# Two output blocks of the w_up product stay in PSUM for the convolution

## The chip, the cores and the metric

The kernel runs on one core of one Trainium2 chip. The time is device microseconds of one launch. TensorE (PE in the profile) multiplies into PSUM banks of 128 partitions by 512 words of fp32; VectorE (DVE), ScalarE (ACT) and GpSimd (POOL) do the rest of the arithmetic on SBUF and, the first two of them, on PSUM; SyncE (SP) issues DMAs.

## The reference

One layer of an encoder: two attentions, then a feed-forward part with a convolution over positions. Batch 1, 1024 positions, 1024 features, 2816 hidden features. The attentions are not touched by the change; the feed-forward part is:

```python
h2 = rmsnorm(x, g_ffn[i]) * (1 + scale2) + shift2
u = depthwise_conv_seq(h2 @ w_up[i], conv_w[i], conv_b[i])   # three taps over positions, 5632 channels
u_val, u_gate = jnp.split(u, 2, axis=-1)
x = x + gate2 * ((jax.nn.gelu(u_gate, approximate=True) * u_val) @ w_down[i])
return rmsnorm(x, g_final)
```

## The kernel before

Activations lie with features on partitions and positions along the free dimension. Every fp32 operand of the feed-forward part is held as two fp32r tiles, hi (rounded) and lo (the remainder), and a product is three matmuls: hi by hi, hi by lo, lo by hi.

`h2 @ w_up` is done in 22 tiles (`FF`, index t). A tile makes 128 value channels and the 128 gate channels that belong to them, at all 1024 positions: four blocks of 128 by 512, block (i, hf) with i = 0 for value, 1 for gate, and hf for the half of the positions. It is a 2 by 2 product in the Strassen-Winograd way: rows are value and gate, the inner index is cut in two halves of four k-tiles, columns are the position halves. So there are seven products instead of eight, in the order of `STEPS` (weights "11", S2, S1, S3, "12", S4, "22" by activations B11, T2, T1, T3, B21, B22, T4), each of 4 k-tiles by 3 matmuls, 84 matmuls a tile (L1204 to L1206 in `products`). "x" and "xb", "T2hi", "wsh", "whi" and the like in the trace are such operands; wsh and wsl are hi and lo of the summed weights S2, S1, S3.

The seven products go into four PSUM banks a, b, c, d (tag "pj", six in all, so the next tile starts in two others). What each step j does when its product is there:

- j = 0, bank a: copied to the SBUF temporary t (ScalarE, L1210); bank a goes on accumulating.
- j = 1, bank b: added to t (VectorE, L1212), which frees b.
- j = 2, bank c: c + t goes into the SBUF temporary v (L1214).
- j = 3, bank d: d + v is block (1, 1), gate, second half (L1217). It is written into v, in SBUF; d is then free.
- j = 4: bank a, with a second product added, is block (0, 0).
- j = 5: bank c with a second product, plus t, is block (0, 1), written in c (L1225).
- j = 6: bank d with a second product, plus t, is block (1, 0), gate, first half (L1229). It is written into t, in SBUF.

So the value row's two blocks are read by the convolution from PSUM, and the gate row's two from SBUF. The temporaries are of `wide()`, an SBUF pool of five tiles called "wc" in the trace.

Each block is handed to `done`. `conv_in` (ScalarE, L1420) starts a row's output y (a "big" tile) with the centre weight and the bias, 512 positions at a time; when both halves are there, `conv_taps` (VectorE, L1426) adds the two side weights in six multiply-adds: two of 512 elements, two of 256, two of 255. For a row whose halves are ph[0] and ph[1], three taps read each. With both rows done come the gelu (ScalarE, L1452), the product (VectorE, L1453) and the store to a DRAM scratch (L1454), from which w_down reads its operand later.

The weights of a tile are loaded two tiles ahead; `a_operands` forms their sums on GpSimd (L1154 to L1156) and one on VectorE (L1171), and splits them: hi on ScalarE (L57), lo on GpSimd (L61).

Two more PSUM banks, tags pcol and pbc, hold the column sums and the broadcast of the RMS norm before w_up (the broadcast, `bc`, is read last by `scale(6)`), and from the w_down stage on they are staging for its operands (`moved`, L1252, which cycles through the two by `stages`).

Tiles 0, 1 and 2 are special: the operand T2, T1, T3 and the others are still being made when they start, so their products run in the order 0, 4, 1, 2, 3, 5, 6 and are interleaved; the convolution of a row waits until both halves are there; tile 2 keeps t and block (0, 0) in two held SBUF tiles. In the last tile (t = 21) things differ too, and the change leaves it out.

The order of instructions on each engine, and which tile takes which buffer, is set when the program is built, by a planner that simulates the engines, except where the kernel is inside `manual_schedule`: there the code's own order holds (PE up to `late_mm.close()` after the first two advances of tiles 0 and 1; ScalarE, VectorE and GpSimd while the operands T2, T1, T3, B22, T4 are made). The taps and the additions of tiles 0 to 21 are outside of these, as is PE from `late_mm.close()` on.

Of the kernel before, what the change touches and what calls it, by code (L numbers as in the profile page):

```python
# [10 lines left out]
FT = mybir.dt.float32  # L11
# [9 lines left out]
FF = 22  # L21
# [8 lines left out]
def hybrid_encoder(tc, xT, c, w_ada, small, w_in, p1_bias, p23_bias, na_bias, ln2_mult, ident, w_br, w_out,  # L30
# [218 lines left out]
    def v_wide(*sts):  # L249
        ps = [ps_s.tile([128, 512], FT, name="pv", bufs=3) if len(sts) == 1 else ps_g.tile([128, 512], FT, name="pj")  # L250
              for _ in sts]
        for k in range(KT):
            whi, wlo = (t[:, :, k] for t in v_all)
            for st, p in zip(sts, ps):
                hhi, hlo = (t[:, st % 4 * 128:st % 4 * 128 + 128] for t in h[st // 4, k])
                pe.matmul(p, hhi, whi, start=k == 0, stop=False)
                pe.matmul(p, hhi, wlo, start=False, stop=False)
                pe.matmul(p, hlo, whi, start=False, stop=k == KT - 1)
        return ps
# [122 lines left out]
    with tc.manual_schedule(engines={e.engine for e in (sp, act, dve, pool, pe)}):  # L382
# [18 lines left out]
        stage = [None, first]  # L401
# [52 lines left out]
        stage = [ps_n.tile([128, 512], FT, name="pcol"), ps_s.tile([128, 512], FT, name="pv", bufs=3)]  # L454
# [45 lines left out]
        for n, step in enumerate(v_steps[:9]):  # L500
            if step is None:
# [3 lines left out]
                ps = [ps_g.tile([128, 512], FT, name="pj") for _ in range(2)]  # L505
# [9 lines left out]
            else:  # L515
                p = v_wide(*step[1:])
# [489 lines left out]
    with tc.manual_schedule(engines={e.engine for e in (pe, act, dve)}):  # L1006
        for s in range(101):
            n = 4 if s < 64 else 8 if s < 72 else 6 if s < 88 else 4
# [23 lines left out]
    ps = tc.alloc_tile_pool(name="ps", bufs=1, space=PSUM, reuse_waits="tile")  # L1032
# [29 lines left out]
    with tc.tile_pool(name="gate", bufs=1, reuse_waits="tile") as work:  # L1062
# [37 lines left out]
        for i in range(2 * KT):  # L1100
# [17 lines left out]
            p = []  # L1118
# [64 lines left out]
        pair(raw[0][:, 1:2], ("S4",), s4[:, 0:1], s4[:, 1:2])  # L1183
        yield

    def products(st, n, moving, done, seq=range(7), in_psum=False, hold=None):

        p, c = {}, {}

        def bank(x_):  # L1190
            p[x_] = ps.tile([128, 512], FT, name="pj", bufs=6)
            return p[x_]

        def tmp(x_):
            c[x_] = hold[0] if hold and x_ == "t" else wide()
            return c[x_]
        for j in seq:
            a, b = STEPS[j]
            x_ = "abcdacd"[j]
            psum = bank(x_) if j < 4 else p[x_]  # L1200
            whi, wlo = st[a]
            for k in range(n):
                bhi, blo = moving(b, k)
                pe.matmul(psum, whi[:, k], bhi, start=j < 4 and k == 0, stop=False, skip_group_check=True)  # L1204
                pe.matmul(psum, whi[:, k], blo, start=False, stop=False, skip_group_check=True)  # L1205
                pe.matmul(psum, wlo[:, k], bhi, start=False, stop=k == n - 1, skip_group_check=True)  # L1206
                if k < n - 1:
                    yield -1
            if j == 0:
                act.activation(tmp("t"), psum, AF.Copy)  # L1210
            elif j == 1:
                dve.tensor_tensor(c["t"], psum, c["t"], OP.add)  # L1212
            elif j == 2:
                dve.tensor_tensor(tmp("v"), psum, c["t"], OP.add)  # L1214
            elif j == 3:
                dst = p["b"] if in_psum else c["v"]
                dve.tensor_tensor(dst, psum, c["v"], OP.add)  # L1217
                done(1, 1, dst)
            elif j == 4 and hold:
                act.activation(hold[1], psum, AF.Copy)  # L1220
                done(0, 0, hold[1])
            elif j == 4:
                done(0, 0, psum)
            elif j == 5:
                dve.tensor_tensor(psum, psum, c["t"], OP.add)  # L1225
                done(0, 1, psum)
            else:
                dst = psum if in_psum else c["t"]
                dve.tensor_tensor(dst, psum, c["t"], OP.add)  # L1229
                done(1, 0, dst)  # L1230
            yield j
# [8 lines left out]
    def wide(dtype=FT):  # L1240
        return keep.tile([128, 512], dtype, name="wc", bufs=5)

    def big(shape, dtype=FT):
        return keep.tile(shape, dtype, name="big", bufs=9)
# [5 lines left out]
    stages = itertools.cycle(("pcol", "pbc"))  # L1250
# [136 lines left out]
    held = [up1.tile([128, 512], FT, name="held", bufs=2) for _ in range(2)]  # L1387
# [25 lines left out]
    with tc.tile_pool(name="up", bufs=2, reuse_waits="tile") as work:  # L1413
# [5 lines left out]
        def conv_in(y, t, hf, src):  # L1419
            act.activation(y[:, halves[hf]], src, AF.Identity, bias=conv[:, 3, t:t + 1], scale=conv[:, 1, t:t + 1])  # L1420

        def conv_taps(y, t, ph):
            w0, w2 = conv[:, 0, t:t + 1], conv[:, 2, t:t + 1]

            def tap(dst, src, wt):
                dve.scalar_tensor_tensor(y[:, dst], src, wt, y[:, dst], OP.mult, OP.add)  # L1426
            tap(slice(256, 768), ph[0], w0)
            tap(slice(768, 1024), ph[1][:, 0:256], w0)
            tap(slice(1, 256), ph[1][:, 256:511], w0)
            tap(slice(0, 256), ph[0][:, 256:512], w2)  # L1430
            tap(slice(256, 768), ph[1], w2)
            tap(slice(768, 1023), ph[0][:, 1:256], w2)

        def up_products(t, st, seq=range(7)):
            u, ys = [{}, {}], {i: big([128, S]) for i in range(2) if t == FF - 1}

            def done(i, hf, src):
                u[i][hf] = src
                if len(u[i]) == 1 and t < 3:
                    return  # L1440
                with tc.high_priority(offset=-300 if t == FF - 1 else 0):
                    finish(i, hf)

            def finish(i, hf):
                if i not in ys:
                    ys[i] = big([128, S])
                for n in range(2) if t < 3 else (hf,):
                    conv_in(ys[i], t + FF * i, n, u[i][n])
                if len(u[i]) == 2:
                    conv_taps(ys[i], t + FF * i, u[i])  # L1450
                if len(u[0]) + len(u[1]) == 4:
                    act.activation(ys[1], ys[1], AF.Gelu_apprx_tanh)  # L1452
                    dve.tensor_tensor(ys[0], ys[0], ys[1], OP.mult)  # L1453
                    sp.dma_start(a_scr[t], ys[0])  # L1454
            return products(st, 4, lambda n, k: late[n][k] if n in late else (ops[n][0][:, k], ops[n][1][:, k]), done,
                            seq, hold=held if t == 2 else None)

        raw[1] = up_load(1)
        prep.append(a_operands(raw.pop(1), 4, s_home, sts[1], dve, spot=extra))
        next(prep[1])  # L1460
        next(prep[1])
        gens = [up_products(t, sts[t], (0, 4, 1, 2, 3, 5, 6)) for t in range(3)]

        def advance(g):
# [77 lines left out]
        for t in range(FF):  # L1542
            nxt = iter(())
            if t + 2 < FF:
                raw[t + 2] = up_load(t + 2)
            if 0 < t < FF - 1:
                nxt = a_operands(raw.pop(t + 1), 4, s_home, sts[t + 1], last=t + 2 == FF,
                                 w_at=None if t == 1 else 0, spot=extra if t == 1 else None)
                next(nxt)
            elif t == 0:  # L1550
                nxt = prep[1]
            for j in gens[t] if t < 3 else up_products(t, sts[t]):
                if j in (((2, 5), (2, 3, 5))[t] if t < 2 else (1, 2, 5)):
                    next(nxt, None)
                if t == FF - 1 and j == 0:
                    more = b_operands(0, movs[0])
                    next(more)
                if t == FF - 1 and j == 2:
                    next(more)
                if t == FF - 1 and j == 3:  # L1560
                    oppool2.release()
                    work2 = tc.alloc_tile_pool(name="down2", bufs=1, side="right", reuse_waits="tile")
                    reserve(work2, [(n + e, 2048, G) for n in ("B11", "T2", "T1") for e in "hl"]
                            + [("T3h", 2048, G), ("T3l", 2048, G)])
                    for _ in range(3):
                        next(more)
# [24 lines left out]
    for n, (g0, q) in enumerate(jobs):  # L1591
# [9 lines left out]
        for j in products(sts[n], G, lambda b, k: movs[g0][b][k], lambda i, hf, src: acc(q + 4 * i, hf, src),  # L1601
                          in_psum=True):
# [20 lines left out]
    with tc.manual_schedule(engines={dve.engine}):  # L1623
        for hf, cs in ((0, slice(0, 512)), (1, slice(0, 256)), (1, slice(256, 512))):
            n = cs.stop - cs.start
            late = []
            for m in range(KT):
                if hf == 0 and m + 2 < KT:
                    end_w[m + 2] = end_weights(m + 2)
                p = ps.tile([128, 512], FT, name="pj", bufs=6)[:, :n]  # L1630
# [140 lines left out]
```

## Time and profile before

| | |
|---|---|
| time, median of 3 runs | 1534.29 us (1532.61 to 1536.65) |
| the profiled execution | 1535.67 us, span 1533.8 us |
| mean granted TensorE clock | 0.99 |
| instructions | 21797 |
| busy: PE, DVE, ACT, POOL | 1494.4, 994.6, 771.6, 774.2 us |
| share of the chain of work that ended last | PE 50%, POOL 8%, DVE 7% |
| DMA | 205.77 MB, mean 134 GB/s |

Instructions of a line are shown as output<-inputs by the program's names, with the shape, so that `big<-wc,sm,big 128x512` is a tap that reads an SBUF block and `big<-pj,sm,big 128x512` one that reads a PSUM block. A row of grouped instructions ends with the busy time and the mean of one in ns. "Granted clock" is the share of TensorE's full clock that the chip gave in a stretch. The w_up tiles lie at about 856 to 1310 us of the span, w_down behind them.

### The profile page before, as it was taken

The page shows a single profiled execution, that of the slowest core. Times are in us where ns is not written, and L with a number is a line of the kernel's source. Part 1 is how long each engine was busy: PE and PEld are TensorE (multiplying, and loading weights), DVE is VectorE, ACT ScalarE, POOL GpSimd, SP SyncE. Part 2 cuts the span into 40 slices and gives each one's busy share as a digit, 9 for nine tenths or more (in the row PEclk, how much of TensorE's full clock was granted, in tenths as well). Part 3 has the DMA queues.
Part 4 walks back from the last instruction along what each step waited for, and adds up shares of the span by engine and source line. Part 5 has one row for each costly group of instructions (what it writes and reads, how often), then busy time and mean ns, then how long its engine had stood idle before and what let it go on. Part 6 is the DMA issues. An engine that isn't in the chain of part 4 may idle for free.

```text
span 1533.8 us, 21797 instructions
## 1 busy us (share of the span) xinstructions
PE 1494.4 (97%) x7740; PEld 1267.5 (83%) x7740; DVE 994.6 (65%) x1892; ACT 771.6 (50%) x1439; POOL 774.2 (50%) x640
## 2 busy tenths in 40 slices
PE   8999999999999999999999989999999998999998
PEld 7888888889798998878888867888888887778787
DVE  5775357575656655646525798766666668787765
ACT  4331566666656566643335463444444447475542
POOL 1021344443335444512268578676666666779721
PEclk9999999999999999999999999999999999999999
DMA  9567333333625456477644222222222224513313
GB/s 349 191 242 258 93 107 82 108 90 102 185 83 150 128 143 173 149 246 234 213 137 147 88 69 96 82 98 88 85 84 86 86 78 154 191 62 124 117 55 111
DMA packets 112725, 205.77 MB, mean 134 GB/s; under 512 B 40516, under 2 KB 53188, under 8 KB 112580
## 3 DMA queue, kind: packets, MB, share of 16 engines
q1 hardware_dynamic: 112344, 204.12, 41.2%
q8 instruction: 61, 1.00, 0.3%
q14 instruction: 48, 0.39, 0.1%
q10 hardware_dynamic: 272, 0.26, 0.1%
HBM read 159.25 MB, written 42.47 MB: 132 GB/s over the span
## 4 chain that ended last, share of the span: by engine, by line
PE 50%; POOL 8%; DVE 7%; ACT 3%; issue 3%; DMA 3%; DVEq 0%; POOLq 0%; ACTq 0%
PE pj L1204 8%; PE pj L1205 8%; PE pj L1206 8%; PE pj L84 6%; PE pj L86 6%; PE pj L85 6%; POOL wsl L61 2%; DMA wraw<-w_down 2%; PE pj L365 2%; PE O L932 2%; POOL wlo L61 2%; DVE big L1426 1%; PE T L919 1%; PE S L897 1%; DVE kl L340 1%
## 5 line engine op out<-in xcount | busy, mean ns | idle before, releaser
L61 POOL TENSOR_TENSOR wlo<-wraw,whi 128x512 fp32r<-128x512 f32 (+1 forms) x94 | 116.1, 1256 | 173.6 <-ACT whi L57 155.4
L84 PE MATMUL pj<-h,whi 128*128 128x512 f32 x448 | 186.7, 417 | 2.6 <-ACT h L207 2.2
L85 PE MATMUL pj<-h,whi 128*128 128x512 f32 x448 | 176.5, 394 | 2.1 <-DVE h L209 2.1
L86 PE MATMUL pj<-h,wlo 128*128 128x512 f32 x448 | 176.3, 393 | 0.0
L61 POOL TENSOR_TENSOR wsl<-big,wsh 128x512 fp32r<-128x512 f32 (+1 forms) x86 | 116.6, 1376 | 43.4 <-ACT wsh L57 43.4
L639 POOL TENSOR_TENSOR wlo<-wraw,whi 128x512 fp32r<-128x512 f32 x58 | 74.7, 1298 | 118.4 <-ACT whi L638 118.4
L589 DVE TENSOR_TENSOR tl<-T,th 128x512 fp32r<-128x512 f32 (+3 forms) x120 | 77.1, 653 | 72.9 <-ACT th L588 71.4
L581 ACT ACTIVATE P<-P,st 128x256 f32<-128x256 f32 x128 | 64.2, 502 | 95.9 <-DVE st L580 95.9
L1426 DVE SCALAR_TENSOR_TENSOR big<-wc,sm,big 128x256 f32<-128x256 f32 (+1 forms) x129 | 101.0, 827 | 15.1 <-ACT big L1420 15.1
L86 PEld LDWEIGHTS pj<-h,wlo 128*128 128x128 f32 x448 | 84.3, 188 | 18.7
L84 PEld LDWEIGHTS pj<-h,whi 128*128 128x128 f32 x448 | 85.0, 190 | 14.3 <-ACT h L207 2.8
L85 PEld LDWEIGHTS pj<-h,whi 128*128 128x128 f32 x448 | 85.0, 190 | 13.4 <-DVE h L209 3.4
L57 ACT ACTIVATE whi<-wraw 128x1024 fp32r<-128x1024 f32 (+2 forms) x51 | 49.5, 972 | 69.8 <-PE pj L85 26.7
L61 POOL TENSOR_TENSOR wsl<-wraw,wsh 128x384 fp32r<-128x384 f32 (+1 forms) x46 | 53.6, 1184 | 58.4 <-ACT wsh L57 58.3
L910 POOL TENSOR_SCALAR P<-P,stb 128x288 f32<-128x288 f32 (+1 forms) x32 | 40.2, 1255 | 72.2 <-DVE stb L907 64.7
L1426 DVE SCALAR_TENSOR_TENSOR big<-pj,sm,big 128x512 f32<-128x512 f32 (+1 forms) x129 | 66.4, 563 | 15.7 <-ACT big L1420 15.7
L588 ACT ACTIVATE th<-T 128x512 fp32r<-128x512 f32 (+3 forms) x120 | 65.6, 566 | 20.4 <-PE T L919 14.0
L57 ACT ACTIVATE wsh<-big 128x1024 fp32r<-128x1024 f32 (+1 forms) x43 | 42.9, 997 | 57.3 <-POOL big L1155 43.0
L547 POOL TENSOR_TENSOR vv<-vv 128x512 fp32r<-128x512 f32 (+1 forms) x40 | 41.9, 1065 | 47.2 <-ACT vv L546 47.2
L580 DVE CUSTOM_DVE_ANT_0 P<-S,bias 128x256 f32<-128x256 f32 x128 | 48.9, 419 | 21.4 <-PE S L692 17.0
L903 ACT ACTIVATE P<-P,stb 128x288 f32<-128x288 f32 (+1 forms) x64 | 36.4, 569 | 50.3 <-DVE stb L901 50.2
L1225 DVE TENSOR_TENSOR pj<-pj,wc 128x512 f32<-128x512 f32 x33 | 22.9, 695 | 53.1 <-PE pj L1206 53.1
(431 smaller groups left out, 4814.3 us busy)
## 6 DMA issues: line engine op xcount, KB each, us to landing
wraw<-w_in SPq DMA_DIRECT2D x34, 512.0 KB, 4.3
wada<-w_ada SPq DMA_DIRECT2D x31, 512.0 KB, 8.0
big<-w_up SPq DMA_DIRECT2D x22, 512.0 KB, 5.4
wraw<-w_up SPq DMA_DIRECT2D x22, 512.0 KB, 3.7
as<-big SPq DMA_DIRECT2D x22, 512.0 KB, 2.8
big<-as SPq DMA_DIRECT2D x22, 512.0 KB, 6.7
wraw<-w_down SPq DMA_DIRECT2D x24, 384.0 KB, 3.6
gs<-gs SPq DMA_DIRECT2D x32, 256.0 KB, 2.9
```

What stands on the lines that cost most here:

```text
L57: act.activation(hi, raw, AF.Copy)
L61: lo_eng.tensor_tensor(lo[:, i:i + step], raw[:, i:i + step], f(hi)[:, i:i + step], OP.subtract)
L84: pe.matmul(psum, whi[:, k0 + k], mhi, start=k == 0, stop=False)
L85: pe.matmul(psum, whi[:, k0 + k], mlo, start=False, stop=False)
L86: pe.matmul(psum, wlo[:, k0 + k], mhi, start=False, stop=k == n - 1)
L588: act.activation(th[:m, :n], pt[:m, :n], AF.Copy)
L589: dve.tensor_tensor(tl[:m, :n], pt[:m, :n], f(th)[:m, :n], OP.subtract)
L639: pool.tensor_tensor(lo[:, i:i + n], raw[:, i:i + n], f(hi)[:, i:i + n], OP.subtract)
L1204: pe.matmul(psum, whi[:, k], bhi, start=j < 4 and k == 0, stop=False, skip_group_check=True)
L1205: pe.matmul(psum, whi[:, k], blo, start=False, stop=False, skip_group_check=True)
L1206: pe.matmul(psum, wlo[:, k], bhi, start=False, stop=k == n - 1, skip_group_check=True)
L1426: dve.scalar_tensor_tensor(y[:, dst], src, wt, y[:, dst], OP.mult, OP.add)
```

## The change

Of each tile but the last, the two gate blocks are no longer written to SBUF. Block (1, 1), of step j = 3, goes into one of the two banks that the norm used, pcol and pbc in turn (called "stage" in the trace, drawn from the same cycle that w_down's `moved` uses later; 21 draws are an odd number, so w_down's first stage is the other one of the two than before). Block (1, 0), of step j = 6, stays where its product was accumulated, in bank d. So bank d is in use until the gate row's taps are done, where before it was free at L1229, and the two norm banks, idle in the w_up tiles before, are in use there. The SBUF temporaries t and v are freed earlier. Arithmetic and number of operations are the same. Lines from 1456 on are numbered two higher.

```diff
-    def products(st, n, moving, done, seq=range(7), in_psum=False, hold=None):
+    def products(st, n, moving, done, seq=range(7), in_psum=False, hold=None, spare=None):
...
             elif j == 3:
-                dst = p["b"] if in_psum else c["v"]
+                dst = p["b"] if in_psum else spare() if spare else c["v"]
                 dve.tensor_tensor(dst, psum, c["v"], OP.add)
                 done(1, 1, dst)
...
             else:
-                dst = psum if in_psum else c["t"]
+                dst = psum if in_psum or spare else c["t"]
                 dve.tensor_tensor(dst, psum, c["t"], OP.add)
                 done(1, 0, dst)
...
             return products(st, 4, lambda n, k: late[n][k] if n in late else (ops[n][0][:, k], ops[n][1][:, k]), done,
-                            seq, hold=held if t == 2 else None)
+                            seq, hold=held if t == 2 else None,
+                            spare=None if t == FF - 1 else
+                            lambda: ps.tile([128, 512], FT, name="stage", tag=next(stages)))
```

The order also moves. On VectorE, where tiles 0 and 1 end (from the second L1225; pj are PSUM banks, wc the SBUF temporaries, big the convolution's output, sm its weights, and TENSOR_SCALAR here is what the trace calls SCALAR_TENSOR_TENSOR), before:

```order
L1225 TENSOR_TENSOR pj<-pj,wc 128x512
L1229 TENSOR_TENSOR wc<-pj,wc 128x512
L1426 TENSOR_SCALAR big<-wc,sm,big 128x255
L1229 TENSOR_TENSOR wc<-pj,wc 128x512
L1426 TENSOR_SCALAR big<-wc,sm,big 128x512
L1426 TENSOR_SCALAR big<-wc,sm,big 128x255
L1426 TENSOR_SCALAR big<-pj,sm,big 128x512
L1426 TENSOR_SCALAR big<-pj,sm,big 128x256
```

and now, where "stage" is a bank of pcol or pbc:

```order
L1225 TENSOR_TENSOR pj<-pj,wc 128x512
L1229 TENSOR_TENSOR pj<-pj,wc 128x512
L1426 TENSOR_SCALAR big<-pj,sm,big 128x512
L1426 TENSOR_SCALAR big<-stage,sm,big 128x255
L1229 TENSOR_TENSOR pj<-pj,wc 128x512
L1426 TENSOR_SCALAR big<-stage,sm,big 128x512
L1426 TENSOR_SCALAR big<-pj,sm,big 128x256
L1426 TENSOR_SCALAR big<-pj,sm,big 128x255
```

The gate taps read PSUM, and the first of them in this place is one of 512 that reads bank d of tile 0, just written by the L1229 ahead of it, where it was one of 255 that reads block (1, 1).

On PE, at the start of tile 2, once the products of tiles 0 and 1 have been issued (T2, T1, T3 are the moving operands, wsh and wsl the weights' parts), before:

```order
L1204 MATMUL pj<-T2hi,wsh 128x512
L1205 MATMUL pj<-T2lo,wsh 128x512
L1204 MATMUL pj<-T1hi,wsh 128x512
L1205 MATMUL pj<-T1lo,wsh 128x512
L1204 MATMUL pj<-T3hi,wsh 128x512
L1205 MATMUL pj<-T3lo,wsh 128x512
L1206 MATMUL pj<-T3hi,wsl 128x512
```

and now:

```order
L1204 MATMUL pj<-T2hi,wsh 128x512
L1205 MATMUL pj<-T2lo,wsh 128x512
L1204 MATMUL pj<-T1hi,wsh 128x512
L1205 MATMUL pj<-T1lo,wsh 128x512
L1206 MATMUL pj<-T2hi,wsl 128x512
L1204 MATMUL pj<-T2hi,wsh 128x512
L1205 MATMUL pj<-T2lo,wsh 128x512
```

Before, the twelve matmuls on T3 stand here, and the other ten on T2 behind them; now those ten on T2 come first, and with them the first use of wsl in this tile, and the twelve on T3 follow.

## The prediction

> **What bounds the kernel now.** I read the page first, then the five stretches that the w_up work falls into, then TensorE's waits in them, then the four engines instruction by instruction in the stretch that loses most.
>
> ```profile
> PE 1494.4 (97%) x7740; PEld 1267.5 (83%) x7740; DVE 994.6 (65%) x1892; ACT 771.6 (50%) x1439; POOL 774.2 (50%) x640
> 856.00:890.00 34.00, 33.63 (x158) 27.62 (x157) 31.12 (x43) 17.66 (x27) 15.69 (x11) 1.00 0.07 24
> 890.00:928.00 38.00, 30.63 (x122) 23.61 (x121) 35.98 (x42) 20.00 (x25) 35.40 (x24) 0.91 0.27 93
> 928.00:1289.00 361.00, 360.89 (x1592) 298.44 (x1592) 254.18 (x368) 161.18 (x203) 252.48 (x191) 1.00 0.26 92
> 1289.00:1310.00 21.00, 16.76 (x64) 12.96 (x63) 20.62 (x33) 17.77 (x31) 13.93 (x14) 0.84 0.34 114
> 1310.00:1534.00 224.00, 211.57 (x1039) 176.68 (x1038) 154.86 (x247) 109.31 (x193) 131.40 (x129) 0.99 0.33 111
> ```
>
> The columns after the length are the busy time of PE, PEld, DVE, ACT and POOL, then the granted clock. From 928 to 1289, nineteen of the 22 tiles, PE is busy 360.89 of 361 us: one matmul each 361/1592 = 0.227 us at full clock. No faster VectorE gives anything there. Two places lose: 890 to 928, where 122 matmuls stand for 38/0.227 = 167 possible (10.3 us lost, clock 0.91, DVE busy 35.98 of 38), and 1289 to 1310. PE's waits from 850 to 1300 name the releasers:
>
> ```profile
> PE pj L1204 <- DVE wc L1214: 3.9, 1, 3.9
> PE pj L1205 <- DVE T1l L1259: 2.7, 1, 2.7
> PE pj L1204 <- ACT wsh L57: 2.4, 2, 1.3
> PE pj L1205 <- DVE T2l L1259: 1.5, 1, 1.5
> PE pj L1206 <- POOL wsl L61: 0.5, 1, 0.5
> ```
>
> **The change, part by part.** First the price of a moved tap (instructions from 880 to 1295, by shape):
>
> ```profile
> L1426 DVE SCALAR_TENSOR_TENSOR big<-wc,sm,big 128x512 f32<-128x512 f32 x41 | 35.9, 877 | 0.0
> L1426 DVE SCALAR_TENSOR_TENSOR big<-wc,sm,big 128x255 f32<-128x255 f32 x42 | 35.8, 851 | 0.1
> L1426 DVE SCALAR_TENSOR_TENSOR big<-wc,sm,big 128x256 f32<-128x256 f32 x42 | 32.5, 777 | 15.1 <-ACT big L1420 15.1
> L1426 DVE SCALAR_TENSOR_TENSOR big<-pj,sm,big 128x512 f32<-128x512 f32 x42 | 31.3, 745 | 15.7 <-ACT big L1420 15.7
> L1426 DVE SCALAR_TENSOR_TENSOR big<-pj,sm,big 128x256 f32<-128x256 f32 x42 | 19.9, 473 | 0.0
> L1426 DVE SCALAR_TENSOR_TENSOR big<-pj,sm,big 128x255 f32<-128x255 f32 x42 | 19.8, 472 | 0.0
> L1426 DVE SCALAR_TENSOR_TENSOR big<-wc,sm,big x129: 468/739/1777, 896.0 to 1298.9; 128x256 f32<-128x256 f32 x43, 128x255 f32<-128x255 f32 x43, 128x512 f32<-128x512 f32 x43
> L1420 ACT ACTIVATE big<-pj,sm x43: 757/763/783, 869.4 to 1288.5; 128x512 f32<-128x512 f32 x43
> L1420 ACT ACTIVATE big<-wc,sm x43: 797/817/819, 895.0 to 1293.3; 128x512 f32<-128x512 f32 x43
> ```
>
> From PSUM every tap costs the same; from wc the shortest is as short (468 ns) but the longest 1777, because POOL is working on SBUF then. Six taps a tile move: 2 x (0.132 + 0.304 + 0.379) = 1.63 us of DVE, 34 us over 21 tiles, and 2 x 0.05 us of ACT. The two additions that now write PSUM (L1217, L1229) I take at the 698 ns of L1225 (mean of 21), which does so already, against 689 and 677: +0.03 us a tile. From 928 on all of this lies beside matmuls and is costed at nothing; the cover is PE itself, which would have to have gaps for it to count.
>
> [...]
>
> What counts is 890 to 928, tiles 0 to 2, where VectorE is behind:
>
> ```profile
> 902.51 0.69 DVE L1225 TENSOR_TENSOR pj<-pj,wc 128x512 f32<-128x512 f32 x1
> 903.82 0.95 DVE L1426 SCALAR_TENSOR_TENSOR big<-wc,sm,big 128x255 f32<-128x255 f32 x1
> 905.34 2.57 DVE L1426 SCALAR_TENSOR_TENSOR big<-wc,sm,big 128x512 f32<-128x512 f32 x2
> 896.99 1.53 DVE L1426 SCALAR_TENSOR_TENSOR big<-pj,sm,big 128x512 f32<-128x512 f32 x3
> 918.67 2.29 DVE L1453 TENSOR_TENSOR big<-big 128x1024 f32<-128x1024 f32 x1
> 922.29 0.68 DVE L1214 TENSOR_TENSOR wc<-pj,held 128x512 f32<-128x512 f32 x1
> 904.50 0.80 ACT L1420 ACTIVATE big<-wc,sm 128x512 f32<-128x512 f32 x1
> ```
>
> In the new order the first gate tap after the second L1225 reads d0 and needs the activation of 904.50, so it starts at 905.3 instead of the 903.82 of the row (DVE idles 1.5 us). From there to L1214 of tile 2 stand 17 taps, six of 512 and eleven short: at the PSUM spacing (0.66 and 0.39, from the row of three at 896.99) 8.3 us. With L1229 0.65, L1453 2.3 beside POOL, L1212 0.65 and L1171 1.2 to 1.7 that is 13.1 to 13.6: L1214 starts at 918.4 to 918.9 and ends at 919.5 at the latest, against 923.0.
>
> PE gains less, since its order changes as well:
>
> ```profile
> 904.65 0.50 PE L1204 MATMUL pj<-T2hi,wsh 128*128 128x512 f32 x1 [1.14 <-ACT wsh L57]
> 909.11 0.50 PE L1206 MATMUL pj<-T2hi,wsl 128*128 128x512 f32 x1 [0.52 <-POOL wsl L61]
> 917.92 0.50 PE L1204 MATMUL pj<-T2hi,wsh 128*128 128x512 f32 x1 [1.27 <-ACT wsh L57]
> 923.02 0.79 PE L1204 MATMUL pj<-x,xb 128*128 128x512 f32 x1 [3.90 <-DVE wc L1214]
> 923.62 0.63 PE L1205 MATMUL pj<-x,xb 128*128 128x512 f32 x1
> 928.29 0.40 PE L1204 MATMUL pj<-B21hi,whi 128*128 128x512 f32 x1
> 899.49 1.30 POOL L1155 TENSOR_TENSOR xb<-xb,wraw 128x512 f32<-128x512 f32 x1
> 903.21 2.71 POOL L61 TENSOR_TENSOR wsl<-wraw,wsh 128x512 fp32r<-128x512 f32 x2 [1.17 <-ACT wsh L57]
> ```
>
> Up to 904.65 nothing on the path moves. From there to the row at 928.29 PE issues 66 matmuls (15.0 us of work) in 23.64: 8.7 lost. In the new order the twelve matmuls on T3 that filled 905.6 to 908.3 come later, because their bank, d0, is kept for its taps; the work on T2 that now stands first needs the low half of its weights, POOL's fourth piece after 903.21. At the 1.25 to 1.30 us that such a piece takes with no VectorE work on two SBUF tiles beside it, that is 908.4; as before it would be 909.1. So PE stands still 2.8 us (to 3.5), not 0.68. I take 2.8, since the taps beside POOL are now those from PSUM. That gap brings the half clock (rows of the stretches where it came and went):
>
> ```profile
> 917.35:920.77 3.42, 1.20 (x4) 0.67 (x4) 3.42 (x3) 2.06 (x3) 3.42 (x3) 0.95 0.01 2
> 920.77:924.18 3.41, 1.16 (x3) 0.96 (x4) 3.41 (x5) 1.15 (x2) 3.41 (x3) 0.50 0.38 154
> 1292.75:1296.20 3.45, 1.38 (x5) 0.48 (x3) 3.45 (x8) 3.45 (x8) 2.21 (x3) 0.96 0.11 13
> 1364.50:1367.90 3.40, 1.80 (x8) 1.50 (x9) 2.68 (x5) 1.48 (x3) 3.40 (x4) 1.00 0.01 2
> ```
>
> Stretches of 3.41 us with PE busy 1.20 and 1.38 were followed by clock 0.50 for 6.8 us, one with 1.80 was not. On the same grid 903.70 to 907.11 would hold four matmuls, 0.9 us. So 907.1 to 913.9 runs at 0.427 us a matmul (spacing of the rows at 923): 13 instead of 24, 2.6 us. The waits at 917.92 and 923.02 and the half clock behind them go: weights ready at 917 and L1214 at 919.5 meet a PE that comes at 920 and 922.3. Lost in all 2.8 + 2.6 = 5.4, against 8.7: **3.3 us gained**. Next late would be L1217 of tile 3, ready about 936.3, wanted about 940.
>
> Edits with one answer: bank d of a tile is next written 96 matmuls (22 us) after its last product, its taps end about 5 us after it; a stage bank waits two tiles. Both hide behind matmuls and cost only if VectorE falls that far behind. The waits of 1289 to 1310 hang on the last tile, which is not changed. The planner also swaps some rows in the w_down stage; by the largest wait there (1.64 us for POOL's wlo at 1366.10) I bound that at -1.6 to +1.6 and take 0. The profiled run took 1535.67 (span 1533.8 and 1.9 around it), 1.4 over the median; the forecast for the median is 1534.3 - 3.3 = **1531.0**.
>
> **The rivals.**
> - *No half clock at 907* (0.26): the 2.6 us are saved, PE then comes to L1214's product at 919.7, just when it is ready: 5.9 us, **1528.4**. For it: the gap is 2.8 us, the stretch's phase may split it. Against it: a gap of 2.7 us (second row of waits) did bring it, and any 3.41 us that begin between 903.0 and 905.9 hold 1.3 us of PE at most. [...]
> - *The gain is given back* (0.16): PE resumes at 909.1 at half clock (2.8 gained), and the w_down swaps and one wait of 1.5 like T2l's cost it: **1534.2**, same.
> - *Slower* (0.10): banks bind. Place: every tile's step on T3, whose bank was freed by the first addition and now waits for the taps. It decides once VectorE ends a tile's gate taps over 17 us late; each us beyond costs 1 us in each of 19 tiles, so one us makes **1550**. Against it: DVE is busy 254 of 361 us and gets 31 us lighter.
>
> **How the numbers follow.** My case has 0.44, its own range 1529.5 to 1532.5. The median of the first kernel can be told to about 0.3% (4.6 us), so faster begins at 1529.7: the first rival and a strip of mine, 0.33; slower needs 1538.9: 0.10; same 0.57. The range takes the first rival with 1.6 us of luck in w_down (1526.8) and the second with a scatter of 1 us (1535.2).
>
> **What would show it.** Taps from stage and pj at 745, 473 and 472 ns; a PE wait of 2.8 us for POOL's wsl near 905.6 with clock 0.5 behind it; no wait for L1214 at 923; PE full until about 1286; the T1l and T2l waits as before, 3 us earlier. Wrong: any PE wait for a tap (L1426) after 930, a clock of 1.00 around 908, or a w_down stage that differs by over 2 us.

## The result, and the profile after

The changed kernel takes 1528.36 us (median of 10 runs, 1524.52 to 1531.65) against 1533.2 for the kernel before (10 runs): a ratio of 0.9966, 95% interval 0.9955 to 0.9977, or 4.8 us less. A second measurement, beside the last experiments, gave 0.9974 (0.9963 to 0.9985). The forecast was 1531.0, range 1526.8 to 1535.2.

The profiled execution of the changed kernel has a span of 1527.8 us, 6.0 less than that of before. The busy engines, and the stretches of w_up and w_down (length, then busy time of PE, PEld, DVE, ACT and POOL, granted clock):

```profile
PE 1496.5 (98%) x7740; PEld 1272.2 (83%) x7740; DVE 963.9 (63%) x1892; ACT 771.9 (51%) x1439; POOL 767.5 (50%) x640
890.00:928.00 38.00, 34.12 (x136) 26.99 (x135) 30.01 (x45) 20.38 (x26) 35.40 (x26) 0.91 0.36 125
928.00:1289.00 361.00, 361.00 (x1595) 299.00 (x1594) 230.81 (x370) 164.52 (x208) 248.30 (x191) 1.00 0.25 89
1289.00:1310.00 21.00, 16.76 (x62) 12.92 (x61) 21.00 (x35) 16.71 (x29) 13.18 (x13) 0.84 0.40 133
```

VectorE is 30.7 us lighter over the span, and 23.4 of it lies between 928 and 1289, where TensorE was full before and is full now. The gain shows in the first row: 136 matmuls instead of 122 between 890 and 928.

What a tap costs now (VectorE's groups by shape, 880 to 1295):

```profile
L1426 DVE SCALAR_TENSOR_TENSOR big<-pj,sm,big 128x512 f32<-128x512 f32 x64 | 47.7, 745 | 18.9 <-ACT big L1420 18.0
L1426 DVE SCALAR_TENSOR_TENSOR big<-pj,sm,big 128x256 f32<-128x256 f32 x64 | 30.3, 473 | 0.0
L1426 DVE SCALAR_TENSOR_TENSOR big<-pj,sm,big 128x255 f32<-128x255 f32 x64 | 30.2, 472 | 0.0
L1426 DVE SCALAR_TENSOR_TENSOR big<-stage,sm,big 128x512 f32<-128x512 f32 x21 | 15.5, 740 | 0.0
```

TensorE at the start of tile 2 (start, duration, and in brackets the idle time before and its releaser):

```profile
904.71 0.50 PE L1204 MATMUL pj<-T2hi,wsh 128*128 128x512 f32 x1 [0.94 <-ACT wsh L57]
905.51 0.40 PE L1205 MATMUL pj<-T1lo,wsh 128*128 128x512 f32 x1
908.30 0.80 PE L1206 MATMUL pj<-T2hi,wsl 128*128 128x512 f32 x1 [2.39 <-POOL wsl L61]
908.89 0.63 PE L1204 MATMUL pj<-T2hi,wsh 128*128 128x512 f32 x1
914.44 0.42 PE L1205 MATMUL pj<-T3lo,wsh 128*128 128x512 f32 x1
922.68 0.39 PE L1204 MATMUL pj<-x,xb 128*128 128x512 f32 x1
```

and VectorE, up to the addition that the last of these rows needs:

```profile
912.78 1.53 DVE L1453 TENSOR_TENSOR big<-big 128x1024 f32<-128x1024 f32 x1
...
916.28 1.00 DVE L1171 TENSOR_TENSOR big<-big 128x512 f32<-128x512 f32 x1
918.80 0.69 DVE L1214 TENSOR_TENSOR wc<-pj,held 128x512 f32<-128x512 f32 x1 [1.52 <-PE pj L1206]
```

The wait of 3.9 us for L1214 is gone: VectorE is free at 917.28, 5 us earlier than before, and itself waits 1.52 us for TensorE. In its place stands the wait of 2.39 us for GpSimd's wsl, with half clock behind it (granted clock 0.50 from 907.66 to 914.48). The transition to w_down is 3.4 us earlier, by the end of its wait for T1l before and now:

```profile
1298.37 0.79 PE L1205 MATMUL pj<-T1l,wsh 128*128 128x512 f32 x1 [2.73 <-DVE T1l L1259]
1295.01 0.80 PE L1205 MATMUL pj<-T1l,wsh 128*128 128x512 f32 x1 [2.73 <-DVE T1l L1259]
```

TensorE's longest waits now, from 850 to 1310 (in all, how many, the longest):

```profile
PE pj L1205 <- DVE T1l L1259: 2.7, 1, 2.7
PE pj L1206 <- POOL wsl L61: 2.4, 1, 2.4
PE pj L1205 <- DVE T2l L1259: 1.5, 1, 1.5
PE pj L1204 <- ACT wsh L57: 0.9, 1, 0.9
```

So by this pair of profiles 3.4 us come from tiles 0 to 2 and 2.6 from behind 1295. The second part is within what two profiles of one kernel differ by, as the experiments show.

### The profile page after: what moved, and what is told of

It is laid out like the page before. It is cut to its first block, busy times and chain, and to the rows that moved or that the text cites. A ratio compares the mean times of both kernels' runs of the same rounds, so it can differ in the third digit from the quotient of the medians.

```text
span 1527.8 us, 21792 instructions
## 1 busy us (share of the span) xinstructions
PE 1496.5 (98%) x7740; PEld 1272.2 (83%) x7740; DVE 963.9 (63%) x1892; ACT 771.9 (51%) x1439; POOL 767.5 (50%) x640
## 4 chain that ended last, share of the span: by engine, by line
PE 57%; DVE 5%; POOL 5%; ACT 3%; issue 2%; DMA 2%; DVEq 0%; POOLq 0%; ACTq 0%
PE pj L1206 10%; PE pj L1205 10%; PE pj L1204 10%; PE pj L84 6%; PE pj L86 6%; PE pj L85 6%; PE pj L365 2%; PE O L932 2%; DMA wraw<-w_down 1%; POOL wsl L61 1%; PE T L919 1%; POOL wlo L61 1%; PE S L897 1%; DVE kl L340 1%; ACT ks L336 1%
## 5 line engine op out<-in xcount | busy, mean ns | idle before, releaser
L61 POOL TENSOR_TENSOR wsl<-big,wsh 128x512 fp32r<-128x512 f32 (+1 forms) x86 | 113.5, 1342 | 47.7 <-ACT wsh L57 47.4
L1426 DVE SCALAR_TENSOR_TENSOR big<-pj,sm,big 128x512 f32<-128x512 f32 (+2 forms) x192 | 99.7, 563 | 18.9 <-ACT big L1420 18.0
L1420 ACT ACTIVATE big<-pj,sm 128x512 f32<-128x512 f32 x64 | 49.2, 772 | 56.5 <-DVE pj L1225 36.2
L1225 DVE TENSOR_TENSOR pj<-pj,wc 128x512 f32<-128x512 f32 x33 | 23.0, 696 | 72.0 <-PE pj L1206 72.0
```

Source lines behind the costliest of these rows:

```text
L61: lo_eng.tensor_tensor(lo[:, i:i + step], raw[:, i:i + step], f(hi)[:, i:i + step], OP.subtract)
```

## The experiments

All are compared with the kernel before on the same chip. For each profile two lengths are worked out: the *w_up part*, from the last matmul ahead of the first on T2 of tile 2 (903.12 before) to the end of the wait for T1l (1298.37 before), and *the rest*, from there to the end of the span. All times in us; the ratio is that of the times, with its 95% interval.

| kernel | ratio | w_up part | the rest | waits of TensorE in tile 2, slow matmuls behind them |
|---|---|---|---|---|
| before | | 395.25 | 235.43 | L1214 3.9, 8 slow |
| changed | 0.9966 (0.9955 to 0.9977) | 391.63 | 232.79 | wsl 2.4, 13 slow |
| e1, tiles 0 to 2 only | 0.9974 (0.9960 to 0.9988) | 390.17 | 236.28 | wsl 2.4, 6 slow |
| e2, tiles 3 to 20 only | 0.9997 (0.9986 to 1.0007) | 394.22 | 233.89 | L1214 3.9, 6 slow |
| e3, block (1,1) only | 0.9966 (0.9954 to 0.9978) | 390.50 | 233.04 | wsh 1.85, 7 slow |
| e4, block (1,0) only | 0.9971 (0.9960 to 0.9982) | 390.97 | 233.43 | wsl 2.6, 8 slow |
| e5, early bank d | 0.9953 (0.9939 to 0.9967) | 388.38 | 235.01 | L1214 1.4, none |
| e6, buffers exchanged | 0.9951 (0.9937 to 0.9965) | 387.65 | 235.27 | L1214 2.4, none |
| e7, the same in the kernel before | 1.0041 (1.0027 to 1.0055) | 400.08 | 235.27 | L1214 9.1, 6 slow |
| e8, VectorE loaded | 0.9988 (0.9978 to 0.9999) | 393.51 | 234.99 | wsl 2.4, 12 slow |
| e9, changed again | 0.9974 (0.9963 to 0.9985) | 398.13 | 234.53 | wsl 2.4, 11 slow; L1212 3.4 |
| e10, e6 again | 0.9951 (0.9934 to 0.9968) | 389.16 | 231.62 | L1214 2.4, 6 slow |
| e11, e6 and L1453 on GpSimd | 0.9947 (0.9930 to 0.9964) | 386.58 | 236.75 | L1214 0.4, none |
| e12, e5 and e6 together | 0.9969 (0.9954 to 0.9984) | 388.90 | 235.10 | L1426 0.5, L1214 3.0, none |

"Slow" are matmuls that follow each other at 0.427 us, as from 908.89 to 914.44 in the changed kernel at granted clock 0.50, instead of 0.227, as from 928 to 1289, so each costs 0.2. e9 is the same kernel as the changed one, and e10 the same as e6. Where a kernel has a line more ahead of them, as e6 and e7, the taps are L1427 in its trace.

**e1 and e2: which tiles.** The change in tiles 0 to 2 alone, and in tiles 3 to 20 alone:

```diff
-                            spare=None if t == FF - 1 else
+                            spare=None if t > 2 else
```

```diff
-                            spare=None if t == FF - 1 else
+                            spare=None if t < 3 or t == FF - 1 else
```

> Only tiles 0, 1 and 2 have their gate blocks in PSUM; tiles 3 to 20 write them to SBUF as before. Theory (the gain comes from the stretch where VectorE is behind, and TensorE is full in the other nineteen tiles): the time is that of the changed kernel, 4 to 6 us under the kernel before, TensorE busy over 360 of 361 us from 928 to 1289, the order of w_down as in the changed kernel. Rival (the taps of all 21 tiles count, 34 us of VectorE lighter): 3 of 21 parts of the gain, under 1 us.

> The other half: tiles 0, 1 and 2 as before, tiles 3 to 20 with their gate blocks in PSUM. Theory: the time of the kernel before, within 1.5 us, with the wait for L1214 at 923 of 3.9 us still there, although VectorE is some 20 us less busy between 928 and 1289. Rival: most of the 4.8 us of gain.

e1 has the gain, 1529.19 against 1533.77; e2 has none, 1533.46. VectorE is lighter where the change was made, and TensorE was full in both (the stretch from 928 to 1285 of e1 and then of e2):

```profile
928.00:1285.00 357.00, 357.00 (x1577) 295.72 (x1575) 246.19 (x365) 163.48 (x208) 251.39 (x190) 1.00 0.26 90
```

```profile
928.00:1285.00 357.00, 357.00 (x1577) 295.84 (x1576) 228.38 (x365) 160.41 (x201) 246.94 (x189) 1.00 0.26 90
```

The 18 us between the two DVE columns are worth nothing, and e2 has the old wait in tile 2:

```profile
920.67 0.79 PE L1204 MATMUL pj<-x,xb 128*128 128x512 f32 x1 [3.89 <-DVE wc L1214]
```

The theory holds and its rival falls, as far as the interval of e2 goes, which leaves 2.1 us at most. e1 issues the same instructions as the changed kernel on TensorE, in tiles 0 to 2 and in w_down, yet its w_up part is 1.5 us shorter and its rest 3.5 longer. That much is spread between executions: e6 and e10, one kernel, have rests of 235.27 and 231.62. The five kernels with TensorE's order of before in w_down (before, e2, e3, e7, e12) have 234.5 on the mean, the five profiles with the new one (changed, e1, e4, e8, e9) 234.4. The 2.6 us of the first pair of profiles are within this spread.

**e3 and e4: which block.** Only block (1, 1) moved, and only block (1, 0):

```diff
-                dst = psum if in_psum or spare else c["t"]
+                dst = psum if in_psum else c["t"]
```

```diff
-                dst = p["b"] if in_psum else spare() if spare else c["v"]
+                dst = p["b"] if in_psum else c["v"]
```

> Block (1,1) goes to a norm bank, block (1,0) goes to SBUF as before. TensorE's order is that of the kernel before in tiles 0 to 2 (T3 first) and in w_down. Theory: no wait of 2.4 us for wsl near 906; half of the gate taps have the price of PSUM, so L1214 of tile 2 ends some 2 us earlier than 923, and TensorE waits about 2 us there instead of 3.9; with the half clock behind it 2 us gained, without it up to 4.5; w_down as before. Rival (the gain of the changed kernel is the other order of w_down, 2.6 us in its profile, and not the taps): no gain.

> Block (1,0) stays in its bank d, block (1,1) goes to SBUF as before. TensorE's order is that of the changed kernel in tiles 0 to 2 (T2 first, T3 waits for the taps of bank d) and in w_down. Theory: the wait for wsl near 906 is there again, 2.4 to 3.2 us, with half clock behind it; L1214 of tile 2 ends 1 to 2 us later than in the changed kernel (919.5), and may be waited for by up to 1.5 us; with w_down as in the changed kernel 3 to 5 us gained. Rival (both blocks must be out of SBUF to get past L1214): 1 us or less in tiles 0 to 2.

Each half gives what the whole gives: 1527.99 for e3, 1529.84 for e4. In e3 L1214 came not 2 but 5 us earlier (before it started at 922.29), and TensorE, which keeps T3 first there, waits for weights instead. VectorE in e3, and then TensorE:

```profile
915.75 1.50 DVE L1426 SCALAR_TENSOR_TENSOR big<-wc,sm,big 128x256 f32<-128x256 f32 x1
917.17 0.68 DVE L1214 TENSOR_TENSOR wc<-pj,held 128x512 f32<-128x512 f32 x1
```

```profile
918.10 0.50 PE L1204 MATMUL pj<-T2hi,wsh 128*128 128x512 f32 x1 [1.85 <-ACT wsh L57]
```

Of the 5 us, 1.1 are L1453, 2.29 us before and 1.22 here. Most of the others are the price of a tap beside GpSimd, which is higher in this place than its mean over all tiles. The kernel before, VectorE's groups from 900 to 923:

```profile
L1426 DVE SCALAR_TENSOR_TENSOR big<-wc,sm,big 128x255 f32<-128x255 f32 x4 | 4.7, 1173 | 0.0
L1426 DVE SCALAR_TENSOR_TENSOR big<-wc,sm,big 128x512 f32<-128x512 f32 x4 | 4.2, 1040 | 0.0
L1426 DVE SCALAR_TENSOR_TENSOR big<-wc,sm,big 128x256 f32<-128x256 f32 x3 | 4.0, 1371 | 0.0
```

These are 0.30 to 0.90 us over the taps from PSUM, not 0.13 to 0.38; the eleven took 12.9 us, and with five of them from a stage bank 9.2 in e3. In e4 the wait for wsl is there again, and L1214 comes at 920.62, in time. Once VectorE is no longer the last, weights are, so moving the second block adds nothing that could be measured.

**e5: the early bank.** Tile 0 alone keeps block (1, 0) in SBUF:

```diff
-                dst = psum if in_psum or spare else c["t"]
+                dst = psum if in_psum or spare and not early else c["t"]
...
+                            early=t == 0)
```

> As the changed kernel, but tile 0 writes its block (1,0) to SBUF, so that bank d of tile 0 is free early and the twelve matmuls on T3 of tile 2 stand first again. Theory: the wait of 2.4 us for wsl near 906 shrinks to under 1 us and the half clock behind it goes, 4.5 us less there; TensorE then comes to the product that needs L1214 of tile 2 at about 915.5 (it stands five matmuls earlier in this order) and waits for it until about 919 to 920, with half clock behind that wait: about the changed kernel's time, within 2 us. Rival (the wsl wait is a loss that nothing takes over): 4 us faster than the changed kernel. The order of w_down is a third one, whose price is open by 2.6 us either way.

As the theory had it, the wait for wsl shrinks (to 0.35 us) and one for L1214 follows; but that one is 1.38 us, shorter than thought, and no half clock comes behind it (granted clock 1.00 from 890 to 928):

```profile
905.62 0.50 PE L1206 MATMUL pj<-T2hi,wsl 128*128 128x512 f32 x1 [0.35 <-POOL wsl L61]
914.55 0.50 PE L1204 MATMUL pj<-x,xb 128*128 128x512 f32 x1 [1.38 <-DVE wc L1214]
```

1525.46 against 1533.85. By the ratios that is 2.0 us better than the changed kernel in its first measurement and 3.2 in its second, with intervals that overlap, and by the w_up part 3.3 (1.8 against e1's). So the time does not decide between the theory's 2 and the rival's 4; the waits are those of the theory, but smaller. That the 2.4 us wait is the price of T2 coming first stands.

**e6 and e7: the weights.** In tile 2 the split weights S2, S1 wait for a buffer that tile 0's last product frees, so ScalarE and GpSimd do S3 first. Both kernels here exchange the two buffers; e6 is built on the changed kernel, e7 on the one before.

```diff
-    s_homes = {n: itertools.cycle([(up1, 2)] * 2 + [None]) for n in ("wsh", "wsl")}
+    s_homes = {n: itertools.chain([(up1, 2), (up1, 2), None, (up1, 2), None, (up1, 2)],
+                                  itertools.cycle([(up1, 2)] * 2 + [None])) for n in ("wsh", "wsl")}
```

> As the changed kernel, but in tile 2 the split weights S2, S1 and S3 exchange their buffers: S2 and S1 take the one that is free after tile 1's T1 step, S3 the one that tile 0's last product frees, so ScalarE and GpSimd make S2, S1 first. Theory (the 2.4 us wait at 906 is the low half of S2 coming as GpSimd's fourth piece): the waits at 904.7 for wsh and at 906 for wsl are gone, TensorE runs to the product that needs L1214 at about 914.8, and VectorE, at L1214 by about 917.0, is waited for by about 2.3 us: 2 to 4 us faster than the changed kernel, 1 us if half clock follows that wait. Rival (the wait at 906 is for the taps that hold bank d, not for the weights): TensorE stands still at 906 as long as before.

> The same exchange of buffers in the kernel before, where the gate blocks are in SBUF. Theory (VectorE's backlog is what the kernel before waits for, so weights that come earlier only lengthen the wait for L1214): L1214 ends at 921 to 923 as before, TensorE waits 5 to 8 us there with half clock behind it, and the time is that of the kernel before within 2 us. Rival (late weights, not VectorE, set the loss of tiles 0 to 2): 3 us or more faster than before.

e6 is at 1526.58, ratio 0.9951; its waits for wsh and wsl are gone and the one for L1214 is the 2.4 us that were expected. e7 is slower than the kernel before, by 6.3 us, where no change within 2 us had been expected: the direction is the theory's, the size is not. Its wait for L1214 of tile 2 is 9.1 us, and tile 4 has one of 2.43 with seven slow matmuls behind it. TensorE in e6, TensorE in e7, VectorE in e7:

```profile
913.08 0.50 PE L1204 MATMUL pj<-x,xb 128*128 128x512 f32 x1 [2.37 <-DVE wc L1214]
```

```profile
923.35 0.79 PE L1204 MATMUL pj<-x,xb 128*128 128x512 f32 x1 [9.13 <-DVE wc L1214]
963.39 0.50 PE L1204 MATMUL pj<-x,big 128*128 128x512 f32 x1 [2.43 <-DVE wc L1214]
```

```profile
903.67 4.60 DVE L1427 SCALAR_TENSOR_TENSOR big<-wc,sm,big 128x255 f32<-128x255 f32 x3
```

TensorE comes to that product at 914.2 and finds VectorE no further than before: it starts L1214 at 922.62, where it was 922.29. Three SBUF taps in a row (the last row), while GpSimd splits weights, take 4.60 us. In tiles 0 to 2 the early weights thus bring the kernel before nothing: 66 matmuls into tile 2's work it is 0.9 us behind. Most of its loss, 3.9 of the 4.8 us in the w_up part, comes in tile 4, where TensorE waits for L1214 again; VectorE's order differs there as well (five SBUF taps stand ahead of L1214 where there were three), and why the loss falls there is not tested. The same early weights make the changed kernel faster (7.3 us in all, 2.3 more than the change alone by the ratios) and the kernel before 6.3 slower. What the change buys in tiles 0 to 2 is VectorE's time there, and how much of it counts depends on when the weights come.

**e8: the cover.** Six copies that nothing reads, on VectorE in tiles 3 to 18 of the changed kernel:

```diff
+                if len(u[i]) == 2 and i == 1 and 2 < t < 19:
+                    spin = wide()
+                    for _ in range(6):
+                        dve.tensor_copy(spin, am1[:, 0:1].to_broadcast([128, 512]))
```

> As the changed kernel, with six extra copies of 128x512 on VectorE behind the gate row's taps in each of tiles 3 to 18 (into a temporary that nothing reads), some 0.5 us each, 3 us a tile. Theory (TensorE is full there and VectorE has 130 of 361 us to spare, bank d is wanted 22 us after its product): the changed kernel's time within 1.5 us, no wait of TensorE for a tap. Rival (the banks that are now held longer bind): TensorE waits for L1426 or L1217 in these tiles, over 3 us in all.

VectorE's costliest group from 928 to 1285, the busy times of that stretch, TensorE's one wait in it, and VectorE ahead of that:

```profile
L1454 DVE COPY wc<-am 128x512 f32<-128x512 f32 x96 | 85.9, 894 | 1.9
```

```profile
928.00:1285.00 357.00, 355.76 (x1568) 293.74 (x1567) 303.74 (x458) 152.56 (x194) 254.52 (x190) 1.00 0.26 89
```

```profile
964.19 0.50 PE L1204 MATMUL pj<-x,wsh 128*128 128x512 f32 x1 [1.24 <-DVE stage L1217]
```

```profile
959.76 3.77 DVE L1454 COPY wc<-am 128x512 f32<-128x512 f32 x3
963.45 0.69 DVE L1217 TENSOR_TENSOR stage<-pj,wc 128x512 f32<-128x512 f32 x1
```

A copy took 894 ns, not the 500 of the author's estimate, so the load was 5.4 us a tile. With VectorE busy 303.74 of 357 us TensorE waited once, 1.24 us, for the addition into a stage bank, which stood behind three of the copies. That is under the rival's 3 us, and no wait is for a tap: that bank d is kept for its taps never binds here. The time, though, is 1532.68, by the ratios 3.4 us over the first measurement of the changed kernel and 2.1 over the second, both above the theory's 1.5; the intervals of the first pair just miss each other, those of the second overlap, so how much it is stays unsure. The w_up part is 1.9 us longer, 1.24 of it that wait; the rest of the span differs by no more than the spread, and what the remainder is the profile does not show.

**e9 to e12: which is best.** The changed kernel and e6 side by side, e6 with one product more on GpSimd, and e6 with e5:

```diff
-                    dve.tensor_tensor(ys[0], ys[0], ys[1], OP.mult)
+                    (pool if t == 0 else dve).tensor_tensor(ys[0], ys[0], ys[1], OP.mult)
```

> The changed kernel itself, beside the next three: 4 to 6 us under the kernel before.

> The changed kernel with the exchange of weight buffers, a second time, beside the changed kernel. Theory (2.8 us at 906 and the half clock behind it are saved, 2.4 us of waiting for L1214 take their place): 2 to 4 us faster than the changed kernel. Rival (the first difference of 2.3 us between their ratios was spread): under 1 us.

> As the one before, and the product of gelu and value of tile 0 (L1453, 2.06 us, on VectorE ahead of L1214 of tile 2) goes to GpSimd. Theory (VectorE's backlog before L1214 is what is left to wait for): L1214 ends 2 us earlier, the wait of 2.4 us for it shrinks to under 0.6 us, 2 us faster than the exchange alone. Rival (GpSimd has no room): its weights for tile 3 come 2 to 2.6 us later and TensorE waits for wlo or wsl of tile 3 instead, no gain.

> The exchange of weight buffers together with tile 0's block (1,0) in SBUF, so that bank d of tile 0 is free early too. Theory: T2's weights are there and nothing waits at 906 in either, so the early bank gives nothing more; three taps of tile 0 are from SBUF beside GpSimd again and cost some 0.5 us each, so L1214 ends 1 to 1.5 us later and is waited for so much longer: 1 to 1.5 us slower than the exchange alone. Rival (the early bank d saves a wait of its own): faster than the exchange alone.

The medians are 1529.88 (e9), 1525.92 (e10), 1525.22 (e11) and 1528.78 (e12), against 1534.01; e9 is 4.1 us under that, as expected. e10 repeats e6's ratio to the last digit, so the exchange is worth 3.5 us to the changed kernel in this measurement and 2.3 in the first; the intervals of each pair overlap, but each of the six runs of e10 is shorter than each of the thirteen of e9. e11 shrinks the wait as expected:

```profile
910.83 0.50 PE L1204 MATMUL pj<-x,xb 128*128 128x512 f32 x1 [0.42 <-DVE wc L1214]
```

and has the shortest w_up part of all, 386.58, but of the 2 us that were expected the medians show 0.7, not to be told from none. e12 waits 2.99 us for L1214 and 0.49 for a tap, 1.1 us more than e10 in all, as expected; its median is 2.9 us longer, and that it is slower is likely and not certain (0.9969 against 0.9951, overlapping).

## Why the prediction was right

- **The bound, and where the gain is: right.** Everything that can be measured comes from tiles 0 to 2 (e1, e2); the 23.4 us that VectorE is lighter from 928 to 1289 do nothing.
- **The taps: right.** 745, 473, 472 ns, and 740 from a stage bank. The 31 us by which VectorE was to get lighter from 928 to 1289 were 23.4. The taps there fell from 145.4 to 118.5 us, 27, since the means for SBUF taps took in the dear ones of tiles 0 to 2; and L1171, whose inputs are still in SBUF, rose from 24.3 to 27.6, which the prediction had not counted.
- **L1214: no longer waited for, as forecast; its time agrees by luck.** It was to start at 918.4 to 918.9 and did at 918.80, but only because it waited 1.52 us for TensorE: VectorE's own work was done at 917.28, over 1 us before the forecast. L1453 took 1.53 us, not 2.3, and L1171 1.00, not 1.2 to 1.7. With L1214 no longer waited for, this cost nothing.
- **The new wait for wsl: right.** It was to end at 908.4 and ended at 908.30, and the gap of 2.8 us from matmul to matmul (905.51 to 908.30) is the one forecast. e5, where T3 is first again, and e6, where the weights come early, are both rid of it.
- **The half clock behind it: right that it comes, the size one draw of several.** Thirteen slow matmuls were forecast and thirteen followed, which is luck. The stretches of 3.41 us around the gap, on about the prediction's grid, in the changed kernel:

```profile
903.73:907.14 3.41, 1.24 (x5) 0.67 (x4) 1.90 (x5) 3.41 (x5) 3.41 (x4) 1.00 0.13 19
907.14:910.55 3.41, 2.25 (x5) 1.83 (x6) 3.41 (x8) 3.39 (x5) 3.41 (x3) 0.58 0.83 276
910.55:913.96 3.41, 3.41 (x9) 2.65 (x8) 3.41 (x6) 2.39 (x3) 3.41 (x4) 0.50 0.03 12
```

  But the same 2.8 us without a matmul were followed by 6 slow ones in e1, 12 in e8 and 11 in e9, 2.75 us by none in e6 and by 6 in e10, and 3.4 us by none in e12:

```profile
917.43 0.50 PE L1204 MATMUL pj<-x,xb 128*128 128x512 f32 x1 [2.99 <-DVE wc L1214]
```

  By the clock in the traces the half clock lasted 6.8 us in the changed kernel (907.66 to 914.48), e8 and e9, and 3.4 us in e1 and e10. The grid of the stretches had been taken over from the kernel before. In that kernel's profile the clock falls at 661.02, 920.43 and 1295.90, 76 and 110 times 3.413 us apart; in the changed kernel's it falls at 661.90, 907.66 and 1293.36, 72 and 113 times 3.413 us apart, but from 907.66 to 920.43 it is 3.74 times, so the grid lies elsewhere there. One kernel also shows different numbers of slow matmuls, 13 and 11 in the two profiles of the changed kernel, none and 6 in those of e6 and e10. So the term can be nothing; where the gap is 2.8 it was 1.2 to 2.6 us (6 to 13 matmuls at 0.2), 2.1 on the mean of the four profiles, and 2.6 was its upper end. Ahead of the half clock the first row above has 1.24 us of TensorE's work, much as the prediction's two such stretches have 1.20 and 1.38.
- **The sum: right in its terms, too small for the first measurement.** 3.3 us were forecast. The 66 matmuls that took 23.64 us take 20.69 now (904.71 to 925.40), 2.9 less, and the w_up part shrank by 3.6 in the first pair of profiles and by 5.1 in e1, which differs in the length of the half clock. The two measured gains are 4.8 and 4.0, with intervals of 3.5 to 6.9 and 2.3 to 5.7. The median of 1531.0 was 2.6 too high, and 1528.36 lies outside the 1529.5 to 1532.5 of the prediction's own case, though inside the range, which took in a rival; the second measurement, 1529.88, is inside both. Of the 2.6 us, 1.1 come from the kernel before, which came out at 1533.2 over ten runs and not at 1534.29, and some 0.5 from the half clock, if the mean of four profiles is taken; the remaining 1 us is not accounted for.
- **The rivals.** "No half clock at 907" gave 1528.4, nearly the measured time, but not for its reason: half clock was there in both profiles of this kernel, and in e1, e4 and e8. "Slower, banks bind" falls with e8: 5.4 us a tile more on VectorE brought no wait for a tap. "Given back" (whose terms add up to 1534.6, not 1534.2) falls, as w_down's new order has no price beyond the spread of 3.5 us between executions; the bound of 1.6 us for it was too tight as a bound on what two profiles can differ by, and by the prediction's own sign (a w_down that differs by over 2 us) one would have looked there for a cause that isn't.

## What to carry to other kernels

A saving on an engine counts only in the stretch where that engine is waited for: here 30.7 us off VectorE gave 4 to 5, as far as can be told all from 3 of 22 tiles, and half of the edit gave as much as the whole. When a wait is removed, look for what is second last (here weights that come in the wrong order because of a buffer): repairing only that lost 6.3 us in the old kernel and gained 2.3 to 3.5 in the new. Compare profiles stage by stage from a common event; two executions of one kernel (e6 and e10) differ by 3.65 us in one stage.

## What the runs showed of the hardware

The price of a tap from SBUF goes with GpSimd. In the trace of the kernel before, 71 of the 129 taps from wc run while GpSimd does nothing; those of 255 and 256 elements take 468 to 487 ns and those of 512 735 to 742, as from PSUM. The other 58 overlap a GpSimd instruction and take up to 1777 ns, on the mean 1070 (short) and 1302 (512). No run took GpSimd away to test it.

Once, a VectorE instruction with two SBUF inputs lasted until GpSimd paused. In the profile of e9, the changed kernel again, the product that takes 1.22 to 1.76 us in its first profile took 11.50. VectorE, GpSimd beside it, and TensorE's longest wait:

```profile
913.32 11.50 DVE L1453 TENSOR_TENSOR big<-big 128x1024 f32<-128x1024 f32 x1
```

```profile
913.73 1.31 POOL L1155 TENSOR_TENSOR big<-big 128x512 f32<-128x512 f32 x1
...
918.71 5.04 POOL L61 TENSOR_TENSOR wsl<-big,wsh 128x512 fp32r<-128x512 f32 x4
```

```profile
PE pj L1204 <- DVE held L1212: 3.4, 1, 3.4
```

GpSimd started eight instructions in that time, one behind the other until 923.75, at 1.30 to 1.33 us each, and the product ended a microsecond later. That one held up the other is read from these times alone. It is why that execution has a w_up part 6.5 us longer than the first profile, and most of why its span is 1536.6 us; in the other profiles the longest of these products took 1.8 to 2.3 us. Taps from PSUM show no such thing: in the trace of the kernel before 126 of the 129 taps from pj overlap a GpSimd instruction, and they took 464 to 478 ns (short) and 735 to 751 (512). What the change really saves is the time of six taps a tile that now have this price; the product and L1171 still read SBUF alone.
